# A macaron trunk layer on one core: the residual kept feature-major from load to store, norms by column sums on TensorE

## The chip, the cores and the metric

The kernel runs on one core of a Trainium2 chip. A core has five engines, each with its own in-order queue: TensorE (PE in the profile; PEld is its loading of the stationary operand), VectorE (DVE), ScalarE (ACT), GpSimd (POOL) and SyncE (SP), which issues most DMA transfers. Only PE multiplies matrices; it writes to PSUM, in banks of 512 fp32 columns by 128 partitions. The metric is device time in microseconds.

## The reference

Input x is 1 x 1024 tokens x 1024 features, fp32. One layer is computed, with the hidden width of the FFNs 2816:

```
rms(x, g) = x * rsqrt(mean(x*x over features) + 1e-6) * g
swiglu(x) = (silu(x @ w_gate) * (x @ w_up)) @ w_down

h = x + 1/2 * swiglu_1(rms(x, g1))
u = rms(h, g2)
[qA|kA|vA|qB|kB|vB|gA|gB] = u @ W_in
h = h + (sigmoid(gA) * (attnA(..) @ W_A) + sigmoid(gB) * (attnB(..) @ W_B)) @ W_out
h = h + 1/2 * swiglu_2(rms(h, g3))
y = rms(h, g4)
```

attnA is a neighbourhood attention on a 16 x 64 grid of tokens, attnB a windowed attention with rotary positions and a sink; the change does not touch them.

## The kernel before

Every matrix product is made of fp32 operands split in two (`split`, lines L89 and L90: ACT writes the high part, DVE subtracts it for the low part) and multiplied by three 128x512 matmuls (`mm3`, L141, L143, L145). The large products are further cut by a Strassen-Winograd scheme into seven half-size products P1 to P7, on half the tokens or features or on sums and differences of such halves.

Stages, in order: norm 1; the gate and up products (`hidden`, driven by `products`), whose results go to DRAM; their down product (class `Down`); the norm in front of the input projection, and that projection; attention A and B; the branch products and the merge; the down product with W_out; a norm and the second FFN; the last norm and the store.

The residual, 1024 x 1024, stands in eight tiles `res(t)`: four `fx` tiles and four quarters of `fa`, each 128 tokens by 1024 features. In `Down` the order of the products is P2, P1, P5, P6, P3, P7, P4. Each product has `n` entries (11 for the FFNs, 4 for W_out), of four times three matmuls; each finished product is added to a 128x512 slot of the residual by DVE (`evict`, L523). The last `TAIL` entries of P4 are left to `tail`, which finishes one column block j after another, so that residual tile 4 is complete first and tile 7 last.

A norm of a tile (`normed`) is one ACT square with a sum along the features (L119), two small POOL steps (add epsilon L122, power -1/2 L123) and one DVE scaling by the root and the gain (L125), of 1024 columns. `turned` then transposes the tile by eight PE transposes into two PSUM banks (L134). `to_strassen` splits those into the operands of the next products: tiles 0 to 3 give B11 and B21 and are copied back transposed (L204, L205); tiles 4 to 7 give T1, T2 and B22 (L209, L211), and the differences for T3 and T4 (L214, L215), which `strassen_rest` splits.

`transition` runs this tile after tile, as a generator: tile t is transposed while tile t+1 is normed. `Down.into` starts it at entry 5n (the first of P7, when the residual of the first four tiles is complete), takes five steps there, and the remaining ones, with the tails of the tiles 4 to 7, when the entries are used up. `behind` puts pieces of the next products between the late tiles: ten block products each. In the last FFN the norm of tiles 0 to 3 is made beside the running product (`finish`), and that of tiles 4 to 7 in parts (`begin`, `rest`, `scale`), so that behind the last matmul only half a tile is left.

The code is not the order on the engines: a list scheduler of the framework places each instruction, by its own estimate, and PE's, DVE's and POOL's queues then run in that order, each instruction waiting for its operands.

## Time and profile before

| | us |
|---|---|
| median of 3 runs | 1955.34 (1954.54 to 1957.08) |
| profiled execution | 1955.32, span 1953.5, granted clock 0.999 |
| PE busy | 1925.7 (99%) |
| DVE busy | 1433.2 (73%) |
| ACT busy | 954.8 (49%) |
| POOL busy | 341.5 (17%) |
| first matmul of three-part products | 22.0 after the start |
| from the last matmul's end to the end | 7.2 |

The span counts from the first to the last recorded instruction; about 1.8 us of the execution lie around it. PE's busy time is modelled: matmuls overlap, so a matmul shown with 0.39 us starts 0.23 us behind the one before. In a row of a timeline stand the start, the length, the engine, the line, the operation, out<-in and the number of instructions taken together; in brackets the idle time before it and what ended it. Three places matter here: the head (0 to about 66 us), the hand-over from the first FFN to the input projection (597 to 700) and that from W_out to the second FFN (1286 to 1356).

### The profile page before, as it was taken

How to read it: one execution, taken by the hardware profiler on the slowest of the kernel's cores; microseconds unless marked ns; L12 is line 12 of the kernel's file. 1: busy time of each engine (PE TensorE's matmuls, PEld its weight loads, DVE VectorE, ACT ScalarE, POOL GpSimd, SP SyncE). 2: the span in 40 equal slices, each digit the busy share in tenths (PEclk: the TensorE clock that was granted, in tenths of full speed). 3: DMA queues.
4: the chain of work that ended last, by engine and by line, in shares of the span. 5: the costliest groups of instructions: out<-in, count | busy, mean ns of one | idle time of the engine just before them, and what ended most of it. 6: DMA issues, size and time to landing. Idle time of an engine off the chain costs nothing.

```text
span 1953.5 us, 25658 instructions
## 1 busy us (share of the span) xinstructions
PE 1925.7 (99%) x8968; PEld 1605.1 (82%) x8968; DVE 1433.2 (73%) x2503; ACT 954.8 (49%) x1850; POOL 341.5 (17%) x469
## 2 busy tenths in 40 slices
PE   7999999999999999999999999999999999999998
PEld 5888888888888888888888888878888888888886
DVE  7875566558967688678888857989666556569864
ACT  7433333334446543467777873366333333344453
POOL 2010001002500112211112135510101001005210
PEclk9999999999999999999999999999999999999999
DMA  6433323367233568653358675544523332393341
GB/s 214 150 111 105 114 87 108 120 220 280 82 119 130 170 177 255 210 183 92 91 148 184 182 233 206 182 141 146 151 87 108 108 103 92 136 362 111 108 145 60
DMA packets 234785, 293.45 MB, mean 150 GB/s; under 512 B 14209, under 2 KB 161025, under 8 KB 234657
## 3 DMA queue, kind: packets, MB, share of 16 engines
q1 hardware_dynamic: 206240, 205.19, 33.7%
q0 software_dynamic: 27840, 85.58, 13.2%
q8 instruction: 71, 1.16, 0.2%
q10 hardware_dynamic: 576, 1.05, 0.1%
q14 instruction: 58, 0.47, 0.1%
HBM read 205.16 MB, written 86.70 MB: 149 GB/s over the span
## 4 chain that ended last, share of the span: by engine, by line
PE 86%; issue 6%; DVE 4%; POOL 2%; DMA 1%; ACT 1%; SPq 0%; POOLq 0%; ACTq 0%; DVEq 0%
PE g L141 16%; PE g L143 16%; PE g L145 16%; PE d L145 10%; PE d L143 10%; PE d L141 10%; PE d L1034 2%; PE d L1013 1%; PE d L1014 1%; PE g L1048 1%; PE g L1053 1%; DVE ws L90 1%; DVE ar L90 1%; PE d L134 1%; DVE ar L1159 1%
## 5 line engine op out<-in xcount | busy, mean ns | idle before, releaser
L141 PE MATMUL g<-ar,ws 128*128 128x512 f32 x1152 | 433.3, 396 | 2.4 <-ACT ar L89 1.6
L143 PE MATMUL g<-ar,ws 128*128 128x512 f32 x1152 | 427.1, 390 | 0.0
L145 PE MATMUL g<-ar,ws 128*128 128x512 f32 x1152 | 425.6, 390 | 0.3 <-DVE ws L90 0.3
L90 DVE TENSOR_TENSOR ws<-raw,ws 128x512 fp32r<-128x512 f32 (+1 forms) x329 | 236.6, 724 | 175.4 <-ACT ws L89 174.1
L89 ACT CAST ws<-raw 128x512 fp32r<-128x512 f32 (+1 forms) x331 | 209.4, 638 | 285.9 <-PE g L145 119.2
L143 PE MATMUL d<-ar,ws 128*128 128x512 f32 x712 | 271.9, 389 | 1.1 <-POOL ar L90 1.1
L141 PE MATMUL d<-ar,ws 128*128 128x512 f32 x712 | 272.3, 390 | 0.5 <-ACT ws L89 0.5
L145 PE MATMUL d<-ar,ws 128*128 128x512 f32 x712 | 271.7, 389 | 0.6 <-DVE ws L90 0.5
L145 PEld LDWEIGHTS g<-ar,ws 128*128 128x128 f32 x1152 | 216.4, 188 | 46.5 <-DVE ws L90 0.7
L143 PEld LDWEIGHTS g<-ar,ws 128*128 128x128 f32 x1152 | 216.6, 188 | 45.6 <-DVE ar L90 0.5
L141 PEld LDWEIGHTS g<-ar,ws 128*128 128x128 f32 x1152 | 211.3, 188 | 41.3 <-ACT ar L89 2.0
L143 PEld LDWEIGHTS d<-ar,ws 128*128 128x128 f32 x712 | 133.6, 188 | 29.0 <-POOL ar L90 1.5
L145 PEld LDWEIGHTS d<-ar,ws 128*128 128x128 f32 x712 | 133.7, 188 | 28.8 <-DVE ws L90 1.0
L141 PEld LDWEIGHTS d<-ar,ws 128*128 128x128 f32 x712 | 133.6, 188 | 28.7 <-ACT ws L89 1.1
L356 POOL DMA_DIRECT2D hid<-fx x96 | 52.1, 542 | 502.6 <-DVE fx L398 380.4
L90 DVE TENSOR_TENSOR ws<-ar,ws 128x512 fp32r<-128x512 f32 x114 | 110.2, 973 | 5.3 <-ACT ws L89 5.3
L89 ACT CAST ar<-raw 128x512 fp32r<-128x512 f32 (+1 forms) x83 | 56.0, 679 | 91.3 <-PE g L143 55.0
L90 DVE TENSOR_TENSOR ws<-fa,ws 128x512 fp32r<-128x512 f32 x76 | 52.5, 691 | 53.4 <-ACT ws L89 52.9
L141 PE MATMUL g<-ws,ws 128*128 128x512 f32 x232 | 90.9, 392 | 0.0
L145 PE MATMUL g<-ws,ws 128*128 128x512 f32 x232 | 90.4, 390 | 0.0
L143 PE MATMUL g<-ws,ws 128*128 128x512 f32 x232 | 90.3, 389 | 0.0
L1021 ACT ACTIVATE fa<-fa,nmx 128x385 f32<-128x385 f32 (+3 forms) x128 | 75.5, 591 | 27.2 <-DVE nmx L1018 26.5
(244 smaller groups left out, 3515.2 us busy)
## 6 DMA issues: line engine op xcount, KB each, us to landing
raw<-hid SPq DMA_DIRECT2D x70, 512.0 KB
hid<-fx POOLq DMA_DIRECT2D x96, 256.0 KB, 2.5
raw<-in_ffn_w_up_dram SPq DMA_DIRECT2D x32, 512.0 KB
ar<-in_ffn_w_down_dram SPq DMA_DIRECT2D x32, 512.0 KB
...
```

Of the source, the lines that this page charges most:

```text
L89: nc.scalar.copy(dst_hi, src)
L90: (eng or nc.vector).tensor_tensor(dst_lo, src, f32v(dst_hi), op=ALU.subtract)
L134: nc.tensor.transpose(pt[:, c * P:(c + 1) * P], xs[:, (half * 4 + c) * P:(half * 4 + c + 1) * P], ident)
L141: nc.tensor.matmul(b, lhs[0], r[0], start=first, stop=False, **kw)
L143: nc.tensor.matmul(b, lhs[0], r[1], start=False, stop=False, **kw)
L145: nc.tensor.matmul(b, lhs[1], r[0], start=False, stop=last, **kw)
L356: nc.gpsimd.dma_start(hid[PRODUCTS.index(p), i], src)
L1013: nc.tensor.matmul(b[:, :nw], un["q"][s], un["kd"][s][:, k0 * P:k1 * P], start=True, stop=False)
L1014: nc.tensor.matmul(b[:, :nw], un["q"][s], un["kl"][s][:, k0 * P:k1 * P], start=False, stop=True)
L1021: nc.scalar.activation(pr, pr, AF.Exp, scale=-1.0, bias=nmx[:, s:s + 1], accum_out=ssum[:, s:s + 1])
L1034: nc.tensor.transpose(pt[:, i * P:(i + 1) * P], un["pr"][s][:, i * P:(i + 1) * P], ident)
L1048: nc.tensor.matmul(o[:, s], un["v"][s][:, un["k0"] + i, :], un["p"][s][:, i], start=i == 0, stop=i == last)
```

## The change

The residual tile is now 128 features by 1024 columns, of which 512 are one half of the features' blocks and 512 the other, so that a slot (`slot_of(t, n)`) holds 128 features of 512 tokens: tiles 0 to 3 hold the first half of the tokens, tiles 4 to 7 the second. The host gives x in this layout and puts the output back. In `Down.multiply` the operands swap roles: the weights' block is the stationary one, the activations move. No tile is transposed. A norm is a class: `add` squares a slot on ACT and adds it to a running sum on DVE or POOL (which of them is an argument, per norm), `root` sums over the partitions by four matmuls with a column of ones, adds epsilon on DVE and takes the power on POOL, `spread` brings the four columns of roots onto all partitions as a 128x512 bank by four PE transposes of a broadcast, and `scale` multiplies a slot by gain (now one value per partition) and root. Each norm covers four tiles, eight slots. The `behind` pieces become 4, 4, and five times 8 block products. The loads of the second group's first weights move ahead of the late half of x. In the last product the tail runs in two column halves of 256, and the norm of the late tokens is made for each.

```diff
     make_identity(nc, ident)
-    nhalf = const.tile([P, 1], F32, name="nhalf")
+    nhalf = const.tile([P, 4], F32, name="nhalf")
     nc.gpsimd.memset(nhalf, -0.5)
+    ones = const.tile([P, 1], F32, name="ones")
+    nc.gpsimd.memset(ones, 1.0)
+    gains = const.tile([P, 4 * NC8], F32, name="gains")
+    nc.scalar.dma_start(gains, norms)
...
+    def slot_of(t, n):
+        return res(t)[:, n * 512:n * 512 + 512]
+    class Norm:
+        def __init__(self, g, eng):
+            self.eng = eng
+            self.g, self.room, self.acc = g, [xs4(), xs4()], None
+            self.free = [self.room[k // 2][:, k % 2 * 512:k % 2 * 512 + 512] for k in range(4)]
+        def add(self, t, n, cols=slice(0, 512)):
+            sq = self.free.pop(0)
+            nc.scalar.activation(sq[:, cols], slot_of(t, n)[:, cols], AF.Square, scale=D ** -0.5)
+            if self.acc is None:
+                self.acc = sq
+                return
+            self.eng.tensor_tensor(self.acc[:, cols], self.acc[:, cols], sq[:, cols], op=ALU.add)
+            self.free.append(sq)
+        def root(self, ks=range(4)):
+            b, n = bank("d"), len(ks)
+            for i, k in enumerate(ks):
+                nc.tensor.matmul(b[:, i:i + 1], self.acc[:, k * P:(k + 1) * P], ones, start=i == 0, stop=True,
+                                 skip_group_check=True)
+            st = [const.tile([P, 4], F32, tag="st", bufs=4, name=nm_("st"))[:, :n] for _ in range(2)]
+            nc.vector.tensor_scalar(st[0], b[:, :n], EPS, None, op0=ALU.add)
+            nc.gpsimd.tensor_tensor(st[1], st[0], nhalf[:, :n], op=ALU.pow)
+            self.st = st[1]
+        def spread(self, ks=range(4)):
+            self.r = bank("d")
+            for i, k in enumerate(ks):
+                nc.tensor.transpose(self.r[:, k * P:(k + 1) * P], self.st[:, i:i + 1].to_broadcast([P, P]), ident)
+        def scale(self, t, n):
+            c = self.g * NC8 + t % 4 + 4 * n
+            y = slot_of(t, n)
+            nc.vector.scalar_tensor_tensor(out=y, in0=y, scalar=gains[:, c:c + 1], in1=self.r, op0=ALU.mult, op1=ALU.mult)
+            return y
...
+    def transition(pre, g, behind, sums):
+        norm = Norm(g, sums[0])
+        for t in range(4):
+            pre(t)
+            for n in range(2):
+                norm.add(t, n)
+        norm.root()
+        norm.spread()
+        yield
+        for n in range(2):
+            for t in range(4):
+                to_strassen(t, n, norm.scale(t, n))
+                if t % 2:
+                    yield
+        norm = Norm(g, sums[1])
+        for t in range(4, NTT):
+            norm.add(t, 1)
+        for t in range(4, NTT):
+            pre(t)
+            norm.add(t, 0)
+        behind(0)
+        norm.root()
+        behind(1)
+        norm.spread()
+        for t in range(4, NTT):
+            for n in range(2):
+                to_strassen(t, n, norm.scale(t, n))
+            behind(t - 2)
+        behind(6)
...
+    def to_strassen(t, n, y):
+        c = t % 4
+        def put(o, src):
             h, l = rhs(o)
...
+            split(h[:, c, :], l[:, c, :], src)
         if t < 4:
...
+            put((B11, B21)[n], y)
             return
...
+        x11, x21 = [slot_of(c, k) for k in range(2)]
+        t1 = slot_of(t, 0)
+        if n == 0:
+            if kept:
+                x12 = main.tile([P, 512], F32, tag="s1", bufs=1, name=nm_("s1"))
+                nc.scalar.copy(x12, y)
+                nc.sync.dma_start(kept[0][c], x12)
+            nc.vector.tensor_tensor(t1, y, x11, op=ALU.subtract)
+            put(T1, t1)
+            return
+        put(B22, y)
+        nc.vector.tensor_tensor(y, y, t1, op=ALU.subtract)
+        put(T2, y)
+        nc.vector.tensor_tensor(x11, y, x11, op=ALU.subtract)
+        nc.vector.tensor_tensor(x21, x21, y, op=ALU.subtract)
...
+            for c in range(4):
+                split(h[:, c, :], l[:, c, :], slot_of(c, n))
...
-            for m in range(2):
+            for m in range(0 if (i, 0) in ahead else 2):
                 ahead[i, m] = main.tile([P, 1024], F32, tag="ws", bufs=8, name=nm_("ahead"))
...
-        def post(t):
-            if t >= 3:
-                drain(run, 10)
-            if t in (3, 4):
-                load_ahead(t - 2)
+        def post(k):
+            if k == 0:
+                load_ahead(1)
+            elif k == 3:
+                load_ahead(2)
+            drain(run, (4, 4, 8, 8, 8, 8, 8)[k])
...
                 put(i, "P1", snap["11", 0])
             elif p in ("P1", "P6", "P5"):
-                c = snap[dict(P1="11", P6="21", P5="22")[p], m] = sn()
+                c = snap[dict(P1="11", P6="21", P5="22")[p], m] = sn(p == "P1" and not i)
...
-        def multiply(self, e, j):
+        def multiply(self, e, j, cols=slice(0, 512)):
             k, p = self.seq[e]
             s, t = self.ent[e]
             b = (self.W if k in ("P1", "P6", "P7", "P4") else self.Y)[j]
             js = slice(j * P, (j + 1) * P)
-            mm3([b], p == 0 and k in ("P1", "P2", "P5"), p == self.n - 1, (s[:, js], s[:, 512:][:, js]),
-                [(t[:, :512], t[:, 512:])], skip_group_check=True)
-        def evict(self, k, j):
+            mm3([b[:, cols]], p == 0 and k in ("P1", "P2", "P5"), p == self.n - 1, (t[:, js], t[:, 512:][:, js]),
+                [(s[:, :512][:, cols], s[:, 512:][:, cols])], skip_group_check=True)
+        def evict(self, k, j, cols=slice(0, 512)):
             w = k in ("P1", "P6", "P7", "P4")
             t = j + (4 if k in ("P5", "P7", "P4") else 0)
             n = 1 if k in ("P5", "P6", "P7", "P3") else 0
-            sl = res(t)[:, n * 512:(n + 1) * 512]
-            nc.vector.scalar_tensor_tensor(out=sl, in0=(self.W if w else self.Y)[j], scalar=self.scale, in1=sl,
+            sl = slot_of(t, n)[:, cols]
+            nc.vector.scalar_tensor_tensor(out=sl, in0=(self.W if w else self.Y)[j][:, cols], scalar=self.scale, in1=sl,
                                            op0=ALU.mult, op1=ALU.add)
         def run(self):
                 if k in ("P7", "P4"):
                     yield e
-        def tail(self, j):
+        def tail(self, j, cols=slice(0, 512)):
             for e in range(len(self.seq) - self.TAIL, len(self.seq)):
-                self.multiply(e, j)
-            self.evict("P4", j)
+                self.multiply(e, j, cols)
+            self.evict("P4", j, cols)
         def into(self, tr, prods):
             last, done = len(self.seq) - self.RING, 0
-            first = min(5 * self.n, last - 1) if self.n > self.RING else last - 1
+            first = 5 * self.n
             for e in self.run():
-                for g in {first: (0, 1), last: (2, 3, 4, 6)}.get(e, ()) if self.n > self.RING else {last: range(7)}.get(e, ()):
+                large = self.n > self.RING
+                for g in {first: (0, 1), last: (2, 3, 4, 6)}.get(e, ()) if large else {last: range(7)}.get(e, ()):
                     if ar[g].dtype != F32R:
                         new_ar(g)
-                if done < 5 and e >= first:
+                if done < 5 and e >= (first if large or not done else last):
                     next(tr)
                     done += 1
                 if e >= last:
...
     def load_x(t):
-        nc.sync.dma_start(res(t), x2[t])
-    load_x(0)
-    gain = load_gain(n1[0])
-    for t in range(1, 4):
+        nc.sync.dma_start(res(t), x[t])
+    for t in range(4):
         load_x(t)
     for m in range(2):
         hg[0](0, m, 0)
+    hg[3](1)
     for t in range(4, NTT):
         load_x(t)
     for m in range(2):
         hg[0](0, m, 1)
-    drain(transition(res, gain, to_strassen, behind(hg), spare=(2, 3)))
+    drain(transition(lambda t: None, 0, behind(hg), (nc.vector, nc.gpsimd)))
     strassen_rest()
     drain(hg[2])
-    h_d = dram.tile([T, D], F32, name="h_d")
...
     def down1(t):
         if t >= 4:
             down.tail(t - 4)
-        nc.sync.dma_start(h_d[t * P:(t + 1) * P, :], res(t))
-        return res(t)
+        nc.sync.dma_start(h_d[t], res(t))
...
     pg = products(lambda i, m, half: w_cols(win[0], groups[i][m][half] * P), NG, store_z, at_end, (2, 3), range(8, 16))
-    down.into(transition(down1, gain, to_strassen, behind(pg), 2), pg)
+    down.into(transition(down1, 1, behind(pg), (nc.vector, nc.vector)), pg)
     kept.clear()
     strassen_rest()
...
     def down2(t):
         if t >= 4:
             merge.tail(t - 4)
...
+        nc.sync.dma_start(h_d[t], res(t))
+    merge.into(transition(down2, 2, behind(hg), (nc.gpsimd, nc.gpsimd)), hg)
     strassen_rest()
     drain(hg[2])
...
+    def finish(norm, t, n, cols=slice(0, 512), eng=nc.sync):
+        c = 3 * NC8 + t % 4 + 4 * n
+        y = slot_of(t, n)[:, cols]
+        nc.vector.scalar_tensor_tensor(out=y, in0=y, scalar=gains[:, c:c + 1], in1=norm.r[:, cols], op0=ALU.mult, op1=ALU.mult)
+        eng.dma_start(out[t][:, n * 512:n * 512 + 512][:, cols], y)
+    norm = Norm(3, nc.vector)
     for n, _ in enumerate(down.run()):
...
+        if n == 1:
+            for t in range(4):
+                for k in range(2):
+                    norm.add(t, k)
+        if n == 3:
+            norm.root()
+        if n == 4:
+            norm.spread()
+        if 5 <= n < 9:
+            for k in range(2):
+                finish(norm, n - 5, k)
+        if n == 11:
+            late = Norm(3, nc.vector)
+            for t in range(4, NTT):
+                late.add(t, 1)
+    for i in range(2):
+        cols = slice(i * 256, i * 256 + 256)
+        for t in range(4, NTT):
+            down.tail(t - 4, cols)
+            late.add(t, 0, cols)
+            if i and t == 4:
+                late.root((0, 1))
+            if i and t == 5:
+                late.spread((0, 1))
+                for u in range(4, NTT):
+                    for k in range(2):
+                        finish(late, u, k, slice(0, 256), (nc.sync, nc.scalar)[k])
+    late.root((2, 3))
+    late.spread((2, 3))
+    for u in range(4, NTT):
+        for k in range(2):
+            finish(late, u, k, slice(256, 512), (nc.sync, nc.scalar)[k])
...
     data = {name: inputs[name] for name in _INS}
+    data["norms"] = np.stack([np.asarray(inputs[name]).reshape(NC8, P) for name in _NORMS]).reshape(4 * NC8, P).T
     data.update(_consts())
     order = np.arange(T).reshape(ROWS, NTT, 8).transpose(1, 0, 2).reshape(-1)
...
+    data["x"] = np.asarray(data["x"])[0, order].reshape(2, 512, 2, 4, P).transpose(0, 3, 4, 2, 1).reshape(NTT, P, D)
     for name, v in data.items():
         a = np.ascontiguousarray(v)
         arrays[f"in_{name}_dram"] = a
```

How the order of instructions moves, at three places. First PE in the hand-over from W_out to the second FFN, where P7 has begun; before:

```order
L143 MATMUL g_11046<-ar_10823 128x512
L145 MATMUL g_11046<-ar_10823 128x512
L141 MATMUL g_11047<-ar_10823 128x512
L143 MATMUL g_11047<-ar_10823 128x512
L145 MATMUL g_11047<-ar_10823 128x512
L134 MATMUL d_11444<-ident,xs_11409 128x128 x4
L134 MATMUL d_11449<-ident,xs_11409 128x128 x4
L141 MATMUL g_11044<-ar_10823 128x512
```

and after, 22 matmuls behind the first of P7:

```order
L159 MATMUL g_10932<-ws_11185,ws_11186 128x512
L155 MATMUL g_10933<-ws_11185,ws_11186 128x512
L134 MATMUL d_11296<-ones,xs_11275 128x1 x4
L157 MATMUL g_10933<-ws_11185,ws_11186 128x512
L159 MATMUL g_10933<-ws_11185,ws_11186 128x512
L155 MATMUL g_10930<-ar_10711 128x512
L144 MATMUL d_11305<-ident,st_11302 128x128 x4
L157 MATMUL g_10930<-ar_10711 128x512
```

Where the transposes of one tile stood, four roots of half the tokens stand now, and four spreads three matmuls behind them. POOL at the same place, before (two small steps for each tile):

```order
L122 TENSOR_SCALAR st_11410<-st_11410 128x1
L123 TENSOR_TENSOR st_11410<-st_11410,nhalf 128x1
L122 TENSOR_SCALAR st_11439<-st_11439 128x1
L123 TENSOR_TENSOR st_11439<-st_11439,nhalf 128x1
L122 TENSOR_SCALAR st_11492<-st_11492 128x1
```

and after:

```order
L127 TENSOR_TENSOR xs_11275<-xs_11275 128x512
L127 TENSOR_TENSOR xs_11275<-xs_11275,xs_11276 128x512 x2
L127 TENSOR_TENSOR xs_11275<-xs_11275 128x512
L127 TENSOR_TENSOR xs_11275<-xs_11275,xs_11276 128x512 x2
L127 TENSOR_TENSOR xs_11275<-xs_11275 128x512
L138 TENSOR_TENSOR st_11302<-st_11301,nhalf 128x4
L127 TENSOR_TENSOR xs_11410<-xs_11410 128x512
```

Seven adds of 512 columns into one sum now stand ahead of the power. DVE in the hand-over from the first FFN to the input projection, where the late tiles come; before:

```order
L523 SCALAR_TENSOR_TENSOR fa<-g_3511,fa 128x512
L125 SCALAR_TENSOR_TENSOR xs_4846<-fa,st_4847,gain_3276 128x1024
L523 SCALAR_TENSOR_TENSOR fa<-g_3512,fa 128x512
L125 SCALAR_TENSOR_TENSOR xs_4869<-fa,st_4870,gain_3276 128x1024
L523 SCALAR_TENSOR_TENSOR fa<-g_3513,fa 128x512
L209 TENSOR_TENSOR fa<-d_4875,fx_75 128x512
L211 TENSOR_TENSOR fa<-d_4880,fa 128x512
L214 TENSOR_TENSOR fx_75<-fa,fx_75 128x512
```

and after:

```order
L541 SCALAR_TENSOR_TENSOR fa<-g_3456,fa 128x512
L127 TENSOR_TENSOR xs_4723<-xs_4723,xs_4724 128x512
L541 SCALAR_TENSOR_TENSOR fa<-g_3457,fa 128x512
L127 TENSOR_TENSOR xs_4723<-xs_4723,xs_4724 128x512
L541 SCALAR_TENSOR_TENSOR fa<-g_3458,fa 128x512
L127 TENSOR_TENSOR xs_4723<-xs_4723 128x512
L137 TENSOR_SCALAR st_4830<-d_4825 128x4
L92 TENSOR_TENSOR ws_4920<-ahead_4808,ws_4920 128x512
L149 SCALAR_TENSOR_TENSOR fa<-fa,gains,d_4849 128x512 x3
L229 TENSOR_TENSOR fa<-fa,fx_79 128x512
```

The first subtraction for the late half (L209, now L229) stood behind the third of four evicts (L523, now L541); it stands behind all four, the last add and the step on the sums.

155 lines of the change are left out of this document (18 added, 137 removed).

## The prediction, made before the change was run

> **What bounds the kernel now.** I read the page first, then what TensorE (PE) waits for, then stretches, then single instructions. Busy times on the page, and PE's waits (total, times, longest, in us):
>
> ```profile
> PE 1925.7 (99%) x8968; PEld 1605.1 (82%) x8968; DVE 1433.2 (73%) x2503; ACT 954.8 (49%) x1850; POOL 341.5 (17%) x469
> ```
>
> ```profile
> PE d L134 <- DVE xs L125: 10.1, 3, 7.9
> PE d L134 <- ACT fx L204: 3.4, 1, 3.4
> PE g L141 <- ACT ar L89: 1.6, 1, 1.6
> ...
> PE d L145 <- DVE ws L90: 0.5, 1, 0.5
> ```
>
> PE is the bound. Its three large waits (15.1 us) belong to the first norm; afterwards it hardly waits, for a split operand from VectorE (DVE, L90) never over 0.5 us. The stretches (length, then PE, PEld, DVE, ACT, POOL busy) show where that is close:
>
> ```profile
> 0.00:24.00 24.00, 9.63 (x38) 7.66 (x39) 12.50 (x15) 16.41 (x30) 6.83 (x19) 1.00 1.00 313
> ...
> 560.00:580.00 20.00, 20.00 (x90) 16.57 (x89) 11.92 (x19) 7.99 (x14) 0.00 (x0) 1.00 0.32 93
> ...
> 670.00:706.00 36.00, 35.31 (x163) 28.71 (x162) 35.88 (x60) 25.03 (x47) 6.62 (x13) 1.00 0.48 160
> ...
> 1340.00:1360.00 20.00, 20.00 (x89) 16.55 (x89) 19.74 (x34) 10.05 (x18) 1.08 (x2) 1.00 0.39 117
> ```
>
> In the first 24 us PE is busy for 9.63. From 560 to 580, 90 matmuls take 20 us, 0.222 each. From 670 to 706 and from 1340 to 1360 DVE is full as well: behind the transitions to the input projection and to the second FFN it has no slack. So the change is to be judged by what it gives PE, and by how late it starts DVE's work there. Single PE instructions (start, length), which I use as marks:
>
> ```profile
> 66.32 0.39 PE L141 MATMUL g<-ar,ws 128*128 128x512 f32 x1
> ...
> 596.72 0.39 PE L141 MATMUL g<-ar 128*128 128x512 f32 x1
> ...
> 597.40 0.39 PE L141 MATMUL g<-ar 128*128 128x512 f32 x1
> ...
> 657.29 1.03 PE L134 MATMUL d<-ident,xs 128*128 128x128 f32 x8
> 658.08 0.48 PE L141 MATMUL g<-ar,ws 128*128 128x512 f32 x1
> ...
> 698.85 0.39 PE L141 MATMUL d<-ar,ws 128*128 128x512 f32 x1
> ...
> 960.87 0.88 PE L1053 MATMUL g<-ws,fx 128*128 128x256 f32 x6
> 961.58 0.34 PE L1013 MATMUL d<-ar,ar 128*128 128x384 f32 x1
> ...
> 1285.84 0.39 PE L141 MATMUL g<-ws,ws 128*128 128x512 f32 x1
> ...
> 1355.70 0.39 PE L141 MATMUL g<-ar,ws 128*128 128x512 f32 x1
> ```
>
> Matmuls of 512 columns start 0.2267 apart (three from 596.72 to 597.40); I use 0.2265. Eight transposes hold PE 0.79 us, about 0.1 each; with the matmul behind them, which starts slowly, 1.02 us or 0.128 each. Six 256-column matmuls take 0.71, 0.118 each. 596.72 and 1285.84 are the first matmuls of P7, where the first-FFN and W_out down products hand over; 66.32, 698.85 and 1355.70 are where the following products reach P6, the second block of P5, and P6.
>
> **What goes.** 192 transposes: 64 in each transition. The 128 of the later two are worth 16.4 us of PE; 24 of the first 64 run after PE is steady, 3.1 us. DVE's scalings keep their columns (24 of 1024 become 48 of 512), ACT loses the copies L204/L205, its squares keep their columns, and four broadcast loads of gains go. ACT's savings gain nothing: it is 49% busy, and PE's waits for it after the head are short. Swapping the operand roles leaves the count and shape of the down matmuls but for the last 60.
>
> **What comes.** Each norm now needs all eight 128x512 slots of a half of the tokens: eight squares (ACT), seven dependent adds, four 128x1 matmuls ("root"), a DVE and a POOL step, four 128x128 spreads, and only then the first scaling. DVE and POOL rows:
>
> ```profile
> 24.06 0.69 DVE L209 TENSOR_TENSOR fa<-d,fx 128x512 f32<-128x512 f32 x1
> ...
> 659.54 0.68 DVE L209 TENSOR_TENSOR fa<-d,fx 128x512 f32<-128x512 f32 x1
> ...
> 699.20 0.68 DVE L90 TENSOR_TENSOR ws<-raw,ws 128x512 fp32r<-128x512 f32 x1
> 699.80 0.68 DVE L294 TENSOR_TENSOR raw<-s,raw 128x512 f32<-128x512 f32 x1
> ...
> 1285.18 2.48 DVE L523 SCALAR_TENSOR_TENSOR fx<-d,fx 128x512 f32<-128x512 f32 x4
> ...
> 1311.30 0.68 DVE L209 TENSOR_TENSOR fa<-d,fx 128x512 f32<-128x512 f32 x1
> ```
>
> ```profile
> L487 POOL TENSOR_TENSOR ar<-ar,ar 128x512 f32<-128x512 f32 x22 | 35.9, 1635 | 35.0 <-DVE ar L484 35.0
> ...
> L123 POOL TENSOR_TENSOR st<-st,nhalf 128x1 f32<-128x1 f32 x28 | 17.8, 634 | 2.3
> ...
> L485 POOL TENSOR_TENSOR ar<-ar 128x512 f32<-128x512 f32 x4 | 7.3, 1834 | 12.4 <-DVE raw L1158 10.0 <-DVE ar L482 2.5
> ...
> L1139 POOL TENSOR_TENSOR fa<-ar,fa 128x512 f32<-128x512 f32 x4 | 5.2, 1303 | 0.1
> ```
>
> Prices: a DVE instruction of 512 columns 0.60 us (start to start, 699.20 to 699.80). A POOL add 1.30 to 1.83; I take 1.75 with the hand-over to the next, nearest to the in-place ones of L487 and L485. A 128x1 fp32 product is not in the trace: at least 0.1 (a transpose of 128 columns), at most 0.35 by three passes of 0.118; I take 0.3, so 1.2 per root, and four spreads 0.5. From root to spread (DVE step, POOL power 0.63) passes about 1.3; where two or three matmuls stand between, PE stands 0.6.
>
> The Trainium skill ("GPSIMD Engine Reference", 3.1 Elementwise) gives a two-input add some 2.6 cycles an element, an estimate of 1.1 us for 512. The rows above say 1.30 to 1.83, so the trace decides; by the Trainium skill's figure each chain of seven below would be 4.5 us shorter.
>
> *W_out to second FFN (t0 = 1285.84).* The last evicts (1285.18) let the chain start at t0+0.6; seven POOL adds end at t0+12.9. PE's order has the root 22 matmuls behind t0, at t0+5.0: it stands 7.9 us (5 at 1.30 each), everything behind it too, and DVE stands in its queue at its step on the sums. The late half: 118 matmuls (26.7) plus those waits, roots and spreads (10.3) put its root at t0+37.0; its own seven adds end about t0+36.6; the spread is over at t0+40.0. Before, the late half's first subtraction ran at 1311.30, t0+25.5. Then 48 DVE instructions at 0.60 stand ahead of the low weights that PE needs (t0+68.8), and 54 matmuls (12.2) behind: P6 at t0+81.0, against 1355.70, t0+69.9. Net **+11.1** with the saved transposes inside; +5 to +15 (adds at 1.30 and no DVE queue, or DVE slowed by the adds).
>
> *First FFN to input projection (t0 = 596.72).* Here DVE does the adds, and 46 matmuls (10.4) stand ahead of the first root: no wait. The tails end at t0+62, the root stands 12 matmuls behind, the spread 12 more: t0+69.2, when DVE begins the late half (before: 659.54, t0+62.8). 65 DVE instructions at 0.60 reach the mark at t0+108.4, against 698.85, t0+102.1. Net **+6.3**, +2 to +10.
>
> *Head.* These rows set its start and its slow clock:
>
> ```profile
> 4.27 1.06 ACT L119 ACTIVATE xs<-fx 128x1024 f32<-128x1024 f32 x1 [2.27 <-DMA fx<-in_x_dram]
> ...
> 10.47 1.06 ACT L119 ACTIVATE xs<-fx 128x1024 f32<-128x1024 f32 x1 [0.24 <-DMA fx<-in_x_dram]
> ```
>
> ```profile
> 22.01 0.80 PE L141 MATMUL g<-ar,ws 128*128 128x512 f32 x1 [1.62 <-ACT ar L89]
> ...
> 25.10 0.63 PE L145 MATMUL g<-ar,ws 128*128 128x512 f32 x1
> 25.53 0.53 PE L141 MATMUL g<-ar,ws 128*128 128x512 f32 x1
> 25.89 0.39 PE L143 MATMUL g<-ar,ws 128*128 128x512 f32 x1
> ```
>
> A load of 512 KB takes 1.55 us (before, four of them, the gain and three tiles, from 4.27 to 10.47). Without the gain the fourth tile lands near 8.9; sums, root and spread bring the first matmul to about 15 instead of 22.01. On SP's queue two loads of coming weights are put ahead of the late tiles and one gain taken away, so those land 1.55 us later. The late half's seven POOL adds start near 18.8, when enough of them are there, and end near 31.1: PE waits some 5 us at that root, and DVE scales the late half from 34.2 (its first subtraction was at 24.06). 66 DVE instructions at 0.60 end at 73.8, where P6 can start: against 66.32 **+7.5**, +3 to +10.
>
> *Last FFN and end.* In the last down product a norm's roots and spreads cost PE 1.2 + 0.5 = **+1.7**, twelve matmuls cover its chain. 120 tails of 256 columns at 0.118 against 60 at 0.2265: **+0.6**; a half root and spread among them **+0.9**. Behind the last matmul:
>
> ```profile
> 1946.42 0.69 DVE L523 SCALAR_TENSOR_TENSOR fa<-g,fa 128x512 f32<-128x512 f32 x1 [0.27 <-PE g L145]
> 1947.14 0.63 ACT L1192 ACTIVATE raw<-fa 128x512 f32<-128x512 f32 x1 [1.02 <-DVE fa L523]
> ...
> 1948.80 0.75 DVE L1208 SCALAR_TENSOR_TENSOR raw<-fa,st,gain 128x512 f32<-128x512 f32 x1 [1.69 <-POOL st L1204]
> 1949.55 0.37 ACTq L1212 DMA_DIRECT2D out_dram<-raw  x1
> ```
>
> Evict 0.7, square 0.7, power and hops 1.0, scale 0.75, then 3.9 for landing to 1953.5: 7.1. Now the evicts queue behind six scalings (ready at +1.0), square and add +1.85, root, power, spread +3.7, eight scalings of 256 columns at about 0.36 to +6.7 (their eight issues over two queues keep that pace, 0.37 each), landing 3.9: +10.6, so **+3.5** (+2.5 to +5).
>
> Sum: 11.1 + 6.3 + 7.5 + 1.7 + 0.6 + 0.9 + 3.5 = **+31.6** on the profiled execution's 1955.32 (span 1953.5 and 1.8 around it), which is the median's 1955.34: 1987. All low ends give +16, all high ends +46.
>
> **Rivals.** (a) *Faster, 1943.* DVE's full stretches hold work that PE does not need by the marks, so the late start costs nothing: then -16.4 in the transitions, head near 57 at P6 (15, 38 us of matmuls from before's 25.9 to 66.3 without transposes, root, spread and slow clock) for -9.3, four roots and spreads +6.8, +1.7 and +5.0: -12.2. For it: PE waits 0.5 us where DVE is 100% busy. Against: the DVE instructions counted stand ahead of those operands in one queue. It decides where under 28% of the delays (12.2 of 43.8) reach PE.
> (b) *Cheap adds, 1980.* POOL adds at the lowest row, 1.30, and without a hand-over: 7 x 0.45 = 3.2 less in each of the two places with POOL chains. For it: the four of L1139; against: those that work in place, as the new ones do. By the Trainium skill's figure for an add, given above, it would be 1978.
> (c) *Slow clock, 1998.* At the start matmuls run at 0.43 (25.10 to 25.53) until 25.8: 3.9 us at half speed from 22.0, 1.9 lost. If each of some six waits of 4 us or more repeats it, +11. Against: after most of them DVE paces anyway. The Trainium skill ("TensorE: Matmul & The Clock Gate", Part 1) has PE fall to half clock after an idle window of about 3.4 us; no row here shows it after the head.
> (d) *No difference:* delays and savings cancel, 1955.
>
> **How the numbers follow.** Forecast 0.63, (a) 0.14, (b) 0.11, (c) 0.09, (d) 0.03. The range goes from 1962, which leaves out (a) and (d), to 2002, which holds (c). This kernel's measurement tells 0.2% (4 us) from no change: faster 0.14, same 0.03, slower 0.83.
>
> **What would show it.** In the new profile: PE waiting some 8 us at a root (L134) for POOL adds near 1291, some 5 near 26; PE waits for DVE (L92) of 4 us around 650 to 700 and 1335 to 1370; L127 on POOL near 1.6; some 10.6 us behind the last matmul. Wrong it would be if PE's waits stay near 15 us in all, or if roots run far over 0.35 each.

## The result, and the profile after

The changed kernel takes 2012.97 us (median; 2010.88 to 2014.82), beside 1955.57 (1954.54 to 1957.08) for the kernel before on the same chip: 1.0293 times as long, interval 1.0275 to 1.0310. The forecast had the sign right and the size wrong: 1987, with a range up to 2002. The profiled execution took 2014.82 (span 2013.0), 59.5 more than the span of before; the forecast had 31.6.

The page's busy times, and the granted clock in 40 slices:

```profile
PE 1940.9 (96%) x8932; PEld 1610.2 (80%) x8932; DVE 1470.1 (73%) x2587; ACT 942.8 (47%) x1810; POOL 347.7 (17%) x428
...
PEclk8999999999999999999999999987999999999999
```

PE has 36 instructions fewer, is busy 15.2 us longer and idle 44.3 longer (72.1 of the span against 27.8). Slices 27 and 28, from 1308 to 1409 us, lie at the hand-over from W_out to the second FFN, and their clock is down; so is that of the first. PE's waits in the kernel after:

```profile
PE d L134 <- POOL xs L127: 15.5, 3, 6.7
PE d L134 <- DVE xs L127: 13.6, 2, 11.5
PE d L159 <- DVE ws L92: 11.3, 7, 3.4
PE d L144 <- POOL st L138: 5.1, 6, 1.7
PE g L159 <- DVE ws L92: 4.3, 3, 2.6
...
PE g L155 <- ACT fa L671: 1.9, 1, 1.9
```

The first row is the wait that the forecast named: roots waiting for POOL's sums. The second is the first root of the head (11.5) and the one behind the last matmul. The third and fifth are the waits for DVE's low parts. Where the time went is read from the marks of the prediction. In the timeline of the kernel after they stand at:

```profile
85.66 0.39 PE L155 MATMUL g<-ar,ws 128*128 128x512 f32 x1
...
616.05 0.39 PE L155 MATMUL g<-ar 128*128 128x512 f32 x1
...
740.91 0.39 PE L155 MATMUL d<-ar,ws 128*128 128x512 f32 x1
...
1315.61 0.39 PE L155 MATMUL g<-ws,ws 128*128 128x512 f32 x1
...
1409.00 0.39 PE L155 MATMUL g<-ar,ws 128*128 128x512 f32 x1
...
2002.31 0.28 PE L159 MATMUL g<-ar 128*128 128x256 f32 x1
```

For the first FFN's hand-over I take the first matmul into a `d` bank behind the late tiles as its end, 714.49 before and 740.91 after; it is the same place of PE's order in both:

```profile
714.49 0.39 PE L141 MATMUL d<-ar,ws 128*128 128x512 f32 x1
```

| stretch (us) | before | after | longer by | forecast |
|---|---|---|---|---|
| head, to P6 | 66.3 | 85.7 | +19.3 | +7.5 |
| first FFN to input projection | 117.8 | 124.9 | +7.1 | +6.3 |
| from there to P7 of W_out | 571.35 | 574.7 | +3.35 | 0 |
| W_out to second FFN, P7 to P6 | 69.9 | 93.4 | +23.5 | +11.1 |
| second FFN, to the end of the last matmul | 590.65 | 593.4 | +2.8 | +3.2 |
| behind the last matmul | 7.15 | 10.6 | +3.4 | +3.5 |

Two stretches carry 24.2 of the 27.9 us that the forecast lacks. Windows of the kernel after in these two (length, then PE, PEld, DVE, ACT, POOL busy, clock, DMA share, GB/s):

```profile
30.00:40.00 10.00, 3.16 (x11) 2.21 (x10) 4.93 (x6) 2.77 (x5) 7.49 (x6) 0.55 0.16 54
...
1320.00:1330.00 10.00, 3.92 (x15) 2.84 (x13) 1.46 (x3) 2.54 (x6) 7.49 (x6) 0.73 0.17 68
1330.00:1340.00 10.00, 9.73 (x36) 7.86 (x36) 8.07 (x12) 5.32 (x9) 1.80 (x3) 0.76 0.01 2
...
1390.00:1400.00 10.00, 6.63 (x17) 4.95 (x17) 10.00 (x18) 2.44 (x4) 0.54 (x1) 0.66 0.25 79
1400.00:1410.00 10.00, 10.00 (x46) 8.24 (x45) 9.12 (x16) 6.24 (x12) 0.54 (x1) 1.00 0.17 57
```

From 1320 to 1330 only POOL works: that is the root's wait. From 1330 to 1340 PE is full again, but does 36 instructions where 1400 to 1410 has 46: the granted clock is 0.76. Single PE instructions show it, behind the root and behind the last wait ahead of P6:

```profile
1326.84 1.87 PE L134 MATMUL d<-ones,xs 128*128 128x1 f32 x8 [6.08 <-POOL xs L127]
...
1332.66 0.63 PE L157 MATMUL g<-ar 128*128 128x512 f32 x1
1333.09 0.63 PE L159 MATMUL g<-ar 128*128 128x512 f32 x1
...
1393.90 0.80 PE L159 MATMUL d<-ar,ws 128*128 128x512 f32 x1 [3.37 <-DVE ws L92]
1394.49 0.63 PE L155 MATMUL d<-ar,ws 128*128 128x512 f32 x1
1394.92 0.63 PE L157 MATMUL d<-ar,ws 128*128 128x512 f32 x1
```

A matmul of 512 columns starts 0.43 behind the one before it (1332.66 to 1333.09, 1394.49 to 1394.92) instead of 0.2265. Over the whole timeline, 91 matmuls of 512 columns start 0.40 us or more behind another such matmul (waits left out) and lose 19.9 us, against 2 and 0.6 before. The rest of PE's bill: the idle time above, and 64 root and 32 spread instructions in place of 192 transposes.

### The profile page after: what moved, and what is told of

Read it like the earlier page. It is cut to its first block, busy times and chain, and to the rows that moved or that the text cites. A ratio compares the mean times of both kernels' runs of the same rounds, so it can differ in the third digit from the quotient of the medians.

```text
span 2013.0 us, 25557 instructions
## 1 busy us (share of the span) xinstructions
PE 1940.9 (96%) x8932; PEld 1610.2 (80%) x8932; DVE 1470.1 (73%) x2587; ACT 942.8 (47%) x1810; POOL 347.7 (17%) x428
## 3 DMA queue, kind: packets, MB, share of 16 engines
q0 software_dynamic: 27840, 85.58, 12.9%
## 4 chain that ended last, share of the span: by engine, by line
PE 78%; issue 10%; DVE 6%; POOL 3%; ACT 2%; DMA 1%; POOLq 0%; SPq 0%; DVEq 0%; ACTq 0%
PE g L159 14%; PE g L155 14%; PE g L157 14%; PE d L159 10%; PE d L157 9%; PE d L155 9%; PE d L1050 2%; POOL xs L127 1%; DVE ar L92 1%; DVE ws L92 1%; PE g L1064 1%; PE d L1029 1%; PE g L1069 1%; PE d L1030 1%; POOL zs_d L649 1%
## 5 line engine op out<-in xcount | busy, mean ns | idle before, releaser
L159 PE MATMUL d<-ar,ws 128*128 128x512 f32 x712 | 275.4, 395 | 11.5 <-DVE ws L92 11.3
L155 PE MATMUL d<-ar,ws 128*128 128x512 f32 x712 | 275.7, 395 | 5.5 <-ACT hs L661 2.9
L157 PE MATMUL d<-ar,ws 128*128 128x512 f32 x712 | 274.7, 393 | 1.1 <-POOL ar L92 1.1
L159 PEld LDWEIGHTS d<-ar,ws 128*128 128x128 f32 x712 | 135.5, 190 | 43.9 <-DVE ws L92 15.7
L155 PEld LDWEIGHTS d<-ar,ws 128*128 128x128 f32 x712 | 135.4, 190 | 36.5 <-ACT ws L91 4.0
L157 PEld LDWEIGHTS d<-ar,ws 128*128 128x128 f32 x712 | 135.4, 190 | 29.7 <-POOL ar L92 1.5
L155 PE MATMUL g<-ws,ws 128*128 128x512 f32 (+1 forms) x240 | 92.1, 384 | 0.9 <-DVE fa L541 0.9
L157 PE MATMUL g<-ws,ws 128*128 128x512 f32 (+1 forms) x240 | 92.2, 384 | 0.0
L159 PE MATMUL g<-ws,ws 128*128 128x512 f32 (+1 forms) x240 | 92.0, 383 | 0.0
L91 ACT CAST ar<-ar 128x512 fp32r<-128x512 f32 x72 | 44.5, 622 | 89.2 <-PE g L157 49.7
```

The costliest lines, as they stand in the source:

```text
L91: nc.scalar.copy(dst_hi, src)
L155: nc.tensor.matmul(b, lhs[0], r[0], start=first, stop=False, **kw)
L157: nc.tensor.matmul(b, lhs[0], r[1], start=False, stop=False, **kw)
L159: nc.tensor.matmul(b, lhs[1], r[0], start=False, stop=last, **kw)
```

## The experiments

My theory (A in the expectations that follow, where no other is given): the waits lie where the forecast put them, and each of more than about 2 us is followed by some 4 us at half clock, which the forecast left out. The rivals: the sums on POOL alone are the loss (then putting them elsewhere ends it); DVE's pace alone, with the clock without effect; and that the transposes had not been worth anything.

**The same dose of waits in the kernel before.** Seven chains of one to seven operations on POOL (a block minus itself, then additions of the zeros that this gives), each ending in a 128x1 matmul that adds zero to a running bank, in the second FFN, where PE otherwise never waits:

```diff
+                if p == "P6" and m == 0 and chains.get(i):
+                    z = xs4()[:, :512]
+                    nc.gpsimd.tensor_tensor(z, c, c, op=ALU.subtract)
+                    for _ in range(chains[i] - 1):
+                        nc.gpsimd.tensor_tensor(z, z, z, op=ALU.add)
+                    nc.tensor.matmul(bks["Y", 0][:, :1], z[:, :P], z[:, :1], start=False, stop=False,
+                                     skip_group_check=True)
...
+    chains.update({3: 1, 4: 2, 5: 3, 6: 4, 7: 5, 8: 6, 9: 7})
```

> The kernel before, with seven waits put into the second FFN's products, where PE never waits and DVE has slack: behind the P6 products of the groups 3 to 9 POOL runs a chain of 1, 2, ... 7 adds of 512 columns, which end in zeros, and a 128x1 matmul of those zeros is added to a bank that is being summed, so that PE waits for the chain. If the scheduler counts an add as some 0.65 us and it takes 1.5, PE waits 0.9 us per add, 1 to 6.5 us, some 24 us in all. Theory A (a wait of about 2.5 us or more throws PE to half clock for some 4 us, on top of the wait): behind the waits of three and more adds 8 to 13 matmuls run at 0.43 us and 1.7 to 3.0 us are lost each time, about 5 x 2.3 = 11 us beside the waits: near 1990. Theory C (only the waits cost; slow matmuls come from something else in the changed kernel): the time grows by the waits alone, near 1980, with no slow matmuls behind them.

Measured 1989.89 (1985.54 to 1991.59), 1.0171 [1.0156, 1.0187]: 34.0 more than before. PE's waits for the chains, in its table of waits:

```profile
PE d L384 <- POOL xs L383: 19.9, 6, 5.0
```

The timeline behind the two shortest of them:

```profile
1494.24 0.38 PE L384 MATMUL d<-xs 128*128 128x1 f32 x2 [1.43 <-POOL xs L383]
...
1495.04 0.39 PE L143 MATMUL g<-ar,ws 128*128 128x512 f32 x1
1495.27 0.40 PE L145 MATMUL g<-ar,ws 128*128 128x512 f32 x1
...
1535.71 0.38 PE L384 MATMUL d<-xs 128*128 128x1 f32 x2 [2.19 <-POOL xs L383]
...
1536.42 0.63 PE L141 MATMUL g<-ar,ws 128*128 128x512 f32 x1
1536.85 0.63 PE L143 MATMUL g<-ar,ws 128*128 128x512 f32 x1
```

Behind 1.43 us the matmuls start 0.23 apart as ever; behind 2.19 they start 0.43 apart, eight of them. The six waits and what followed:

| wait, us | 1.43 | 2.19 | 3.19 | 3.85 | 4.29 | 4.95 |
|---|---|---|---|---|---|---|
| slow matmuls behind it | 0 | 8 | 9 | 8 | 7 | 12 |
| us lost by them | 0 | 1.65 | 1.60 | 1.59 | 1.45 | 2.49 |

So the slow clock follows a wait in a place without any norm, and costs 8.8 us on top of 19.9 of waiting; of the remaining 5.3 I followed only the seven matmuls themselves (about 0.25 each). The measurement is as Theory A had it (near 1990).

It is not the length of a wait alone that decides. In all eleven traces the granted clock changes only in steps of 3.41 us: the starts of its stretches lie whole multiples of 3.41 us apart, and up to the last matmul half clock lasts one to four such pieces. Around the wait of 2.19 us (length, then PE, PEld, DVE, ACT, POOL busy, clock, DMA share, GB/s):

```profile
1532.66:1536.07 3.41, 1.22 (x7) 0.74 (x6) 2.06 (x2) 0.00 (x0) 2.84 (x3) 1.00 0.18 52
1536.07:1539.48 3.41, 3.41 (x10) 2.63 (x10) 0.69 (x1) 1.10 (x2) 0.00 (x0) 0.50 0.03 5
1539.48:1542.90 3.42, 3.42 (x17) 2.81 (x16) 2.05 (x3) 1.25 (x2) 0.00 (x0) 1.00 0.00 0
```

Laid out over the eleven traces on this grid, from each trace's first piece at full clock on: behind a piece at full clock in which PE, by the rows' modelled ends, idled 1.78 us or more, the next was always at half clock (47 of 47); behind one with less than 1.58 us it never was (0 of 6149); in between, 7 of 14. So a wait that falls into two pieces can pass: the same wait of 2.16 us, of the same statement, brought half clock in the kernel without chain and with 14 zeros (below), where nearly all of it lay in one piece, and none in the same kernel without the zeros, where it lay in two, 1.42 us of it in the second. And a wait of 1.84 us standing alone, in the kernel before with every transpose twice (below), was followed by nine slow matmuls. The Trainium skill ("TensorE: Matmul & The Clock Gate", Part 1) states an idle window of about 3.4 us; the length of the window agrees with the 3.41 us here, but it need not be idle throughout: 1.78 us in it was enough, and the measurement decides.

**Filling waits in the changed kernel.** 11 and 14 matmuls with zero operands stand ahead of the two waits for DVE's low parts in the W_out hand-over. They add work for PE, but in time in which it would wait:

```diff
+        for _ in range(fill):
+            nc.tensor.matmul(banks[0], zr.to_broadcast([P, P]), zr.to_broadcast([P, 512]), start=False, stop=False, **kw)
...
+    fills.update({(1, 'P1', 0): 11, (2, 'P1', 1): 14})
```

> The changed kernel, with 11 and 14 matmuls of zeros ahead of its two longest waits for DVE in front of the second FFN (2.63 us at the first block of P1 in the second group, 3.37 at the second block of P1 in the third); the waits at the roots stay. Theory A: PE leaves both waits at full clock; behind the second nothing else is waited for up to P6, so those 54 matmuls take 12.4 us instead of 15.1 and the hand-over is 2.5 to 3 us shorter, more if the first one counts as well: near 2010. Theory C: 15.1 us as before, 2013.

Measured 2007.63 (2006.48 to 2008.12), 1.0264 [1.0247, 1.0281]: 5.3 less than the change itself, with 25 matmuls more. The timeline of this kernel behind the second of the two waits:

```profile
1388.12 0.50 PE L168 MATMUL d<-ar,ws 128*128 128x512 f32 x1 [1.23 <-DVE ws L96]
1388.45 0.40 PE L162 MATMUL d<-ar,ws 128*128 128x512 f32 x1
1388.69 0.39 PE L164 MATMUL d<-ar,ws 128*128 128x512 f32 x1
...
1400.49 0.39 PE L162 MATMUL g<-ar,ws 128*128 128x512 f32 x1
```

What had been 3.37 us of waiting and slow matmuls is 1.23 and matmuls at full speed: from 1388.12 to P6 at 1400.49 pass 12.4 us, near the forecast's 12.2, instead of 15.1 (1393.90 to 1409.00). And the end of DVE's work ahead of it comes earlier: low weights 74.2 us behind the first matmul of P7 (1313.95 here), instead of 78.3, most of it (3.7) behind the late root. Up to there the order on PE, DVE, ACT and POOL is the same in both, but for the zeros and their making, so this is no reordering. Slow matmuls also cost time while DVE paces: in the changed kernel ACT's copy of a product waits for PE,

```profile
1378.23 0.59 ACT L392 COPY fa<-g 128x512 f32<-128x512 f32 x1 [2.31 <-PE g L159]
```

and DVE then waits 1.41 and 1.12 us for casts that stand behind such copies in ACT's queue; with the zeros that copy waits 0.24, and DVE 0.12 and nothing. The hand-over is 86.5 us instead of 93.4. Part of these 6.9 us is chance: in the run "The end in one piece" below, with the same order here and no zeros, it took 90.8, with 35.6 from the late root to the low weights (36.9 in the changed kernel, 33.2 here) and 15.1 from there to P6. The kernel's time, 5.3 less, is clear of that.

**Sums on DVE.** The three norms whose sums POOL adds (late half in the head, both halves ahead of the second FFN) get DVE:

```diff
-    drain(transition(lambda t: None, 0, behind(hg), (nc.vector, nc.gpsimd)))
+    drain(transition(lambda t: None, 0, behind(hg), (nc.vector, nc.vector)))
...
-    merge.into(transition(down2, 2, behind(hg), (nc.gpsimd, nc.gpsimd)), hg)
+    merge.into(transition(down2, 2, behind(hg), (nc.vector, nc.vector)), hg)
```

> The running sums of the late norm in the head and of both norms in front of the second FFN are made by DVE instead of POOL; nothing else is changed. Theory A (PE waits for the sums, and its clock falls to half after each longer wait): at the hand-over from W_out the seven adds take 4.2 us instead of 10.4, the first root's wait of 6.1 us and the slow matmuls behind it (4 us) go nearly, the second root's 2.7 and the slow ones behind it (3 us) in part; in the head the wait of 6.7 us at the second root falls to about 2, with 2.5 us of slow matmuls: about 17 us less than the changed kernel's 2013, near 1996. Theory B (DVE sets the pace of both places, the waits at the roots are only where that shows): 4.2 us more of DVE work per norm stand in its full stretches, so at most half of that is won: 2004 or above.

Measured 1997.48 (1995.98 to 1998.35), 1.0213 [1.0197, 1.0228]: 15.5 less than the change, as A had it. PE's waits of this kernel:

```profile
PE d L159 <- DVE ws L92: 13.5, 9, 3.4
...
PE g L155 <- DVE fa L541: 4.6, 2, 3.8
```

No wait of a root for POOL is left, and in the W_out hand-over 20 matmuls (counted as above) lose 4.2 us instead of 48 and 10.4. The hand-over costs 11.8 more than before, instead of 23.5. The head still costs 14.4 more. So POOL's sums with what follows them are worth 15.5 of the 57.4 us, not all of it; and since the forecast had waits of 7.9 and some 5 us for them, this does not say how much of what it lacked is theirs.

**A norm without chain.** The norm does away with adds, roots and spreads: a matrix of ones multiplies each square (fp32r, on PE), the eight products accumulate in one bank, and ACT takes the reciprocal root out of it:

```diff
-            self.eng.tensor_tensor(self.acc[:, cols], self.acc[:, cols], sq[:, cols], op=ALU.add)
+            nc.tensor.matmul(self.b[:, cols], ones.to_broadcast([P, P]), sq, start=first, stop=True, skip_group_check=True)
...
+            nc.scalar.activation(self.r[:, cols], self.b[:, cols], AF.Abs_reciprocal_sqrt, bias=epsb)
```

> A norm without adds, roots and spreads: each squared slot, rounded to the fast fp32 form, is multiplied by a stationary matrix of ones, eight matmuls of 512 columns that add up in one bank and give the sum of squares on every partition; ACT takes the reciprocal root of that bank (epsilon as its bias) and DVE scales as in the changed kernel. 8 x 0.23 = 1.8 us of PE per norm against 1.3 for roots and spreads, no POOL, 4.2 us less of DVE. Theory A (chain of sums, waits at the roots, slow clock): PE waits for nothing at the norms, DVE begins the late halves 5 to 10 us earlier; of the 59 us, the hand-over from W_out (23.5) falls to about 5, the one before to 2, the head (19.3) to about 8, the end (4.8) to 3: near 1975. Theory B (DVE's pace alone): the waits at DVE stay, the gain is the 4.2 us a norm and the earlier start: near 1988.

Measured 1981.86 (1980.42 to 1985.16), 1.0136 [1.0121, 1.0151]: the fastest version with a transposed residual, and still 26 us slower than before; between the two expectations. The head costs 6.8 more than before, the first FFN's hand-over 4.6, that of W_out 5.5. PE's waits:

```profile
PE d L155 <- DVE ws L96: 8.8, 4, 3.4
PE d L133 <- ACT xs L132: 7.5, 7, 5.0
PE g L151 <- ACT ar L95: 5.2, 2, 3.6
PE g L155 <- DVE ws L96: 4.3, 3, 2.6
```

The waits for DVE's low parts are about the same as after the change: no chain of adds stands ahead here, but DVE's work still begins only when a whole half of the tokens is summed. That this is what keeps the remaining 26 us is argued, not tested.

**Relieving DVE, on the kernel without chain.** Two of the Strassen differences go to POOL:

```diff
-        nc.vector.tensor_tensor(x11, y, x11, op=ALU.subtract)
-        nc.vector.tensor_tensor(x21, x21, y, op=ALU.subtract)
+        nc.gpsimd.tensor_tensor(x11, y, x11, op=ALU.subtract)
+        nc.gpsimd.tensor_tensor(x21, x21, y, op=ALU.subtract)
```

> The kernel with norms by a matrix of ones (1981.9), where the eight differences that update the early slots for T3 and T4 in each late half are made by POOL instead of DVE (4.8 us of DVE in each of three places; POOL takes some 1.6 us for each, beside). Theory B (what is left of the waits, 2 to 3.4 us at a low part of weights in each place, is DVE's pace): the waits behind fall by up to 4.8 us in each place and the half clock behind them goes too: 12 to 18 us less, near 1967. If POOL slows DVE while it works by as much as it takes over (single DVE subtractions beside POOL took 0.97 instead of 0.70): no gain, 1982.

Measured 1990.30 (1989.10 to 1990.67), 1.0176 [1.0159, 1.0193]: 8.4 slower than without it, a miss for both expectations. Its waits:

```profile
PE d L155 <- DVE ws L96: 8.0, 4, 3.6
...
PE d L151 <- ACT hs L376: 7.0, 3, 2.9
```

Those for DVE hardly fall (8.0 for 8.8), and those for ACT's copy of a product (L376) grow from 1.4 to 7.0. POOL takes 2.44 and 1.66 us for the two differences that took DVE 0.68 each, and DVE's own first difference (L225) takes 0.89 on average instead of 0.68, as the second expectation had feared. So it isn't settled by this run what DVE's pace alone costs.

**Filling one wait, on the kernel without chain.** 14 zero matmuls as above, for one transition's entry:

```diff
+    fills = {(2, "P1", 1): 14}
```

> The same kernel with norms by a matrix of ones (1981.9), with 14 matmuls of zeros (512 columns, 3.2 us) put ahead of the matmul that waits longest for DVE, the low part of the second block of P1 in the third group, in each of the three places (waits 3.36, none, 3.24 us there); the order is otherwise kept, and no wait for data gets shorter. Theory A (half clock behind the wait, on the path because nothing waits between it and P6): PE comes out of the wait at full clock, the 2.7 and 2.5 us lost in the head and in front of the second FFN go, in the middle place the zeros cost up to 3.2 us if nothing waited: 1980 to 1977, and in the trace those two places are 2.5 us shorter each. Theory C (clock not on the path): both places unchanged or longer.

Measured 1984.15 (1981.60 to 1986.28), 1.0145 [1.0130, 1.0160]: no gain, and a miss for Theory A's time. At the place in front of the second FFN it did what was expected: the wait fell from 3.24 to 1.19, no slow matmul followed, and from the low weights to P6 passed 12.4 us instead of 14.8. In the head the zeros came ahead of an earlier wait instead, and 3.1 us with 2.8 lost behind it stayed; and between the input projection and W_out a wait of 3.2 for a scaled copy by ACT stood that the other trace does not have; that stretch (740.91 to 1315.61 in the changed kernel) took 579.9 us instead of 572.6. What brings that wait is open.

**Filling the roots' waits.** 27 and 12 zero matmuls ahead of the roots in the W_out hand-over:

```diff
+            for _ in range(self.fill):
+                nc.tensor.matmul(b, zr.to_broadcast([P, P]), zr.to_broadcast([P, 512]), start=True, stop=True,
+                                 skip_group_check=True)
...
-    merge.into(transition(down2, 2, behind(hg), (nc.gpsimd, nc.gpsimd)), hg)
+    merge.into(transition(down2, 2, behind(hg), (nc.gpsimd, nc.gpsimd), (27, 12)), hg)
```

> In front of the second FFN, 27 matmuls of zeros (512 columns, 6.1 us) stand ahead of the first root and 12 (2.7 us) ahead of the second, so that PE works while POOL adds; what is computed is the same and no wait gets shorter. Theory A (the slow clock after the waits is on the path): the matmuls behind the two roots run at 0.23 instead of 0.43 us, 4.0 and 3.2 us of slow running go, and that hand-over gets about 7 us shorter: near 2006. Theory B (DVE sets the pace, and slow matmuls only use up its lead): what follows the first root counts, since the second half's sums wait for PE's tails, but behind the second root DVE paces: 4 us, near 2009. Theory C (the clock does not matter, or does not depend on PE's idling): no change, 2013, with the slow matmuls still there.

Measured 2012.64 (2011.23 to 2013.29), 1.0289 [1.0272, 1.0306]: nothing gained, and not a clean test. The order of the work counts the zeros as work, so that the first root stands fewer matmuls behind P7 (the zeros come behind some 12 matmuls instead of 22), and PE still waits 2.72 us there, with slow matmuls behind it. The second root's wait was gone, with full speed behind it, but the tails and with them the second sums came later (spread 48.3 us behind the start of P7 instead of 43.8).

**The end in one piece.** The last product's tail and norm in whole slots instead of two column halves:

```diff
...
+    for t in range(4, NTT):
+        down.tail(t - 4)
+        late.add(t, 0)
+    late.root()
+    late.spread()
     for u in range(4, NTT):
         for k in range(2):
-            finish(late, u, k, slice(256, 512), (nc.sync, nc.scalar)[k])
+            finish(late, u, k, slice(0, 512), (nc.sync, nc.scalar)[k])
```

> In the last product the tails run over 512 columns at once and the late norm is made once, behind the last matmul. By single rows: tails 13.6 us instead of 15.05, with no half root and spread among them; behind the last matmul evict 0.7, square 0.6, add 0.6, root 0.9, epsilon and power 1.5, spread 0.4, eight scalings of 512 columns at 0.6 = 4.8 and 3.9 for the last transfer: 13.4 us instead of 10.6. So 1.3 us slower than the changed kernel, if the cutting in halves is worth what its rows say; if the small instructions cost more than they save, the same or faster.

Measured 2013.39 (2011.93 to 2014.21), 1.0294 [1.0279, 1.0309]: the same as the change. In the traces the end is 3.2 longer (15.2 us behind the last matmul instead of 10.6, the tails 1.4 shorter), but the W_out hand-over, where nothing differs, took 90.8 instead of 93.4. The order of work there is the same in both, so that place moves by 2.6 us between these two executions, and the total says nothing on a term of this size.

**What a transpose was worth.** The kernel before with every transpose done twice:

```diff
-            for c in range(4):
+            for c in (0, 1, 2, 3, 0, 1, 2, 3):
```

> The kernel before, with every transpose of a residual tile made twice into the same bank (192 more, the result the same). It measures what one set is worth where it stands. If PE is the bound at the transitions, the 128 of the two later ones cost 128 x 0.1 to 0.128 = 13 to 16 us and those of the head 3 to 6: 16 to 22 us, near 1975. If DVE paces those stretches and PE has room, much less: under 8 us, so that their removal could win little there whatever came in their place.

Measured 1975.93 (1975.31 to 1977.58), 1.0103 [1.0088, 1.0118]: 20.1 more, and the page of this kernel has PE busy for 20.8 more than before:

```profile
PE 1946.5 (99%) x9160; PEld 1627.4 (82%) x9160; DVE 1435.1 (73%) x2503; ACT 956.0 (48%) x1850; POOL 338.6 (17%) x469
```

That is 0.105 us for each of the 192, and it reaches the end; in the trace it includes a wait of 1.84 us for ACT at 1330.89 with its nine slow matmuls. Adding a set is not the same as removing one, but it bears out that PE has no room there: the saving counts, and the price of the change is larger.

## Why the prediction was wrong in size

*What held.* The sign, and the reason that the forecast gave against rival (a): the transposes are worth some 16 to 20 us, and that is less than what the norm over a whole half brings. In the hand-over from the first FFN the spread is over at t0+69.9 (forecast 69.2), and the forecast's own mark (698.85 before, 723.24 after) stands at t0+107.2 (108.4; its 65 x 0.60 gives 108.2), so +5.1 for 6.3; the +7.1 of the table holds 1.5 us of waiting for ACT behind that mark. PE's wait of 2.90 us for ACT there, with eight slow matmuls behind the next wait, the forecast did not have. The last down norm, the tails and the end (+6.2 for 6.7) came out near their terms. The end as the DVE rows show it:

```profile
2002.61 0.75 DVE L541 SCALAR_TENSOR_TENSOR fa<-g,fa 128x256 f32<-128x256 f32 x2
...
2006.81 3.22 DVE L1196 SCALAR_TENSOR_TENSOR fa<-fa,gains,d 128x256 f32<-128x256 f32 x8 [1.30 <-PE d L144]
```

The last matmul ends at 2002.42 (its start and one pitch); the eight scalings begin 4.4 later (forecast 3.7) and end at +7.6 (6.7), with the end of the span at +10.6 as forecast. The roots' waits were found where they were put: 6.08 us ahead of the second FFN (forecast 7.9), and 6.7 in the head (forecast 5). PE's groups and POOL's, for the prices:

```profile
L127 POOL TENSOR_TENSOR xs<-xs,xs 128x512 f32<-128x512 f32 x12 | 18.9, 1579 | 5.8 <-ACT xs L123 5.1
L127 POOL TENSOR_TENSOR xs<-xs 128x512 f32<-128x512 f32 x9 | 14.1, 1563 | 45.8 <-ACT xs L123 45.4
...
L134 PE MATMUL d<-ones,xs 128*128 128x1 f32 x64 | 10.6, 284 | 29.0 <-POOL xs L127 15.5 <-DVE xs L127 13.6
...
L138 POOL TENSOR_TENSOR st<-st,nhalf 128x4 f32<-128x4 f32 x7 | 8.7, 1241 | 169.1 <-DVE st L137 169.1
```

An add takes 1.57 us, between rival (b)'s 1.30 and the 1.75 taken; a root, eight PE instructions here, 0.8 to 0.9 at full clock and 1.7 at half, to the start of the next instruction (1.2 taken; no run shows the three passes of that price, each product of one column stands as two instructions); the power of four columns 1.24 instead of 0.63.

*What failed in the W_out hand-over (+12.4).* The step is "P6 at t0+81.0", with its 118 and 54 matmuls at 0.2265 each: a clock that stays up through the waits which the same sum contains. The slow clock stood only as rival (c), at 0.09, with the sentence that DVE paces anyway. By its own stations, in us behind the first matmul of P7:

| station | forecast | after | after, waits for DVE filled |
|---|---|---|---|
| first root | 12.9 | 11.2 | 11.2 |
| late root | 37.0 | 41.4 | 40.9 |
| low weights | 68.8 | 78.3 | 74.2 |
| P6 | 81.0 | 93.4 | 86.5 |

From the first root to the late one 6.1 us are missing: 2.3 of slow matmuls, 2.67 of a second wait for POOL's sums, which the forecast had ready just ahead of the root, and most of the rest a root and spread at half clock. From the late root to the low weights 5.1: DVE's instructions keep their 0.60 us (0.66 for the scalings), but DVE idles 5.7 us, 2.3 of them for the spread, 2.8 for ACT's casts and 0.6 for a product, beside half clock behind the late root and behind the wait at 1373. From the low weights to P6 2.9: the slow matmuls behind the wait of 3.37. Filling the two waits takes back 5.3 us of the kernel's time; that part is shown by experiment. The part ahead of the late root is read from the trace only, since the run that filled the roots' waits moved the order.

*What failed in the head (+11.8).* Here, as far as the trace tells, the clock is the smaller part. The first matmul stands at 17.68 instead of 15. The steps "the late half's seven POOL adds start near 18.8" and "end near 31.1" are the ones that fail; POOL's rows show the chain:

```profile
22.01 3.01 POOL L127 TENSOR_TENSOR xs<-xs 128x512 f32<-128x512 f32 x1 [7.00 <-ACT xs L123]
...
28.79 1.79 POOL L127 TENSOR_TENSOR xs<-xs,xs 128x512 f32<-128x512 f32 x1 [1.85 <-ACT xs L123]
...
35.66 1.26 POOL L127 TENSOR_TENSOR xs<-xs 128x512 f32<-128x512 f32 x1
```

It starts 3.2 later. The late tiles are issued behind more weight loads (10.43 instead of 6.49 on SP's queue, 3.9 us and not 1.55), but no square of theirs waits for a load in the trace. The second of them, at 21.31, stands in ACT's queue behind a cast that waits for DVE's scaling of the early half:

```profile
20.79 0.62 ACT L91 CAST ar<-fx 128x512 fp32r<-128x512 f32 x1 [1.31 <-DVE fx L149]
```

So the early half's lateness is handed on, where the forecast had the loads decide. The chain takes 14.9 instead of 12.3, with POOL waiting for ACT's squares and ACT for POOL to free one of four square buffers. It ends at 36.9. The root and spread at half clock put DVE's late scalings at 41.7 instead of 34.2 (+7.5), and the remaining 4.3 lie in DVE's stretch and the 54 matmuls behind it, of which 1.7 is slow clock behind the wait at 71.67. No run changed the clock alone here. With the sums on DVE the head is 5.0 shorter; without any chain it is at +6.8, near the forecast's +7.5.

*What the forecast did not have (+3.35).* Between the first FFN's hand-over and W_out, where the change edits little, PE waits 1.9 us at 830 for a scaled copy of a product by ACT (L671), and shorter at other places. At the same statement the kernel without chain and with 14 zeros waited 3.2, and the one without zeros did not. In the changed kernel with the two waits filled, whose order is the same up to there, the stretch is only 1.4 longer than before, so that up to 2 us of the 3.35 vary from execution to execution. The cause is open.

*The chances.* Rival (c) was nearest to the truth, and its price, +11 in all, was still too low: it multiplied one start-up's 1.9 us by six waits of 4 us or more. Behind the start only two waits are that long (6.74 and 6.08), and shorter ones brought half clock too; the trace has slow matmuls worth 19.3 more than before, though not all of that reaches the end. The range's high end of 2002 was set to hold that rival; the high ends of the terms, which the forecast adds up to +46, come to +43.
